# A hybrid transformer block on one core: the modulation product moved from the first mixer (TensorE) to the first MLP (VectorE), a third PSUM bank for the mixer's projections, later closing transposes of the first head, and matmuls on ones at the start

## The chip, the core and the metric

The kernel runs on one core of a Trainium2 chip. The core has five engines with an instruction queue each, which run in order: TensorE (PE, matrix products, with its weight loads shown as PEld), VectorE (DVE), ScalarE (ACT), GpSimd (POOL) and SyncE (SP, which here issues the DMA transfers). An instruction waits at the head of its queue until the semaphores that it needs are set, and everything behind it waits too. The metric is the device time of one execution in microseconds (us); lower is better.

## The reference

All data is fp32: `x` is 512 tokens by 1024. The reference is three stages one after the other:

```python
x = LN(alpha * x + mixer_gdn(x));  x = LN(alpha * x + mlp(x, 0))     # layer 0
x = LN(alpha * x + mixer_gla(x));  x = LN(alpha * x + mlp(x, 1))     # layer 1
mod   = silu(c) @ w_mod + b_mod         # one row of 3072: shift, scale, gate
mod_c = silu(c_ctx) @ w_mod + b_mod     # the same weights, 1024 x 3072
h  = rms(x)   * (1 + scale)   + shift
hc = rms(ctx) * (1 + scale_c) + shift_c  # ctx: 256 tokens
y = branches(h @ w_in, attention over hc and h) @ w_out;  out = x + gate * y
```

`mixer_gdn` is a gated delta rule with 8 heads in both directions: projections to q, k, v and z, a convolution of five taps over the tokens, triangular inverses within chunks of 64 tokens, a scan over chunks, a gated norm and an output projection. `mlp` is `relu(x w1)^2 w2` with 4096 hidden columns. The two modulation rows depend on `c`, `c_ctx` and `w_mod` alone, and nothing needs them before the context's normalisation, which runs beside the first MLP.

## The kernel before, in words

Products of fp32 are made as three products of halves: each operand is split into a rounded part (`hi`) and a rest (`lo`), and `mm3` (lines 337 to 339) issues hi·hi, hi·lo and lo·hi into one PSUM bank. A weight comes as a 512 KB transfer into `raw` on SP's queue (L322), ACT writes `hi` (L310), POOL, or for the mixer's projections VectorE, subtracts to give `lo` (both L316).

The program is written with a framework that fixes the order of every engine's queue ahead of time, from the order in which instructions are emitted and from priorities. `Weave` runs generators in the background of a main generator: at each `yield` of the main one (a tick) each background generator advances at its own rate.

The first mixer, `gdn`, takes 0 to 521 us of the profiled span. Its main generator is `dense(h)` for heads 0 to 7, which runs the projections: `proj` makes 24 matmuls of 128x512 into one of two banks (`acc`), and `proj_conv` then reads that bank with one ACT and four VectorE instructions (L705, `y<-acc`), the convolution; only then is the bank free. In the background stand, for each head, `inverse(h)`: 31 steps of two short POOL instructions (L830 and L832; VectorE does them for head 7), closed by two VectorE transposes (L839, L843) which are pinned in program order; then `double(h)`, `scan(h, d)` (short matmuls `psw`, `pso`, `psr` with VectorE or ACT steps between), and `closing(h)` with `stats` and `finish`. The last head's `finish(7)` (L974, L977) runs within the second half of the output projection (`wout_half`).

`mod`, which makes the two modulation rows, is one more background generator, at rate 0.18 from head 1 on: 24 weights of 512 KB through `wload`, 96 matmuls of 128x512 (L1374) into a bank of their own (`psmod`, the one `held` bank), and per sixth of the row a copy by ACT (L1377), four VectorE transposes (L1382) and two additions (L1385, L1386).

The first MLP takes 521 to 880 us. `mlp` runs 8 blocks of `up` (four columns of 128 hidden units: 24 matmuls, `relu` on ACT, square on VectorE at L485, split on ACT and VectorE) and `wout_half` (whose results VectorE adds at L364 and L366, `zacc<-sm`). A generator `side` is advanced by `next(side, None)` five times per block; it holds `ctx_tile` (which needs the modulation) and `gla_consts`. Then follow `gla` (880 to 1200), the second MLP (1200 to 1545) and the attention block (to the end).

Of the kernel before, what the change touches and what calls it, by code (L numbers as in the profile page):

```python
# [7 lines left out]
F32 = mybir.dt.float32  # L8
# [134 lines left out]
def _prep(inputs):  # L143
    g = {k: np.asarray(v) for k, v in inputs.items()}
    A = {}
    A["cst"] = _consts()
    A["chunk"], A["blocks"] = _chunk(), _blocks()
    x = g["x"][0]
    A["x"] = np.ascontiguousarray(x.reshape(4, 128, 1024).transpose(1, 0, 2))
    A["xT"] = np.ascontiguousarray(x.T.reshape(8, 128, 512).transpose(1, 0, 2))  # L150
    wa = g["a_w_in"][0]
    w4 = wa[:, :4096].reshape(1024, 4, 8, 128)
    w4 = w4[:, [1, 0, 2, 3]].transpose(0, 2, 1, 3).reshape(1024, 4096)
    A["wa"] = _lay_in(np.ascontiguousarray(w4))
# [12 lines left out]
    wb = g["b_w_in"][0]  # L167
    wk, wq = (wb[:, o:o + 512].reshape(1024, 4, 1, 128) for o in (512, 0))
    wr = wb[:, 2048:3072].reshape(1024, 4, 2, 128)
    A["wb"] = _lay_in(np.ascontiguousarray(np.concatenate([wk, wq, wr], 2).reshape(1024, 2048)))  # L170
    A["wbv"] = np.ascontiguousarray(wb[:, 1024:2048].reshape(2, 4, 128, 4, 256).transpose(3, 0, 2, 1, 4))
    A["wgl"] = np.ascontiguousarray(wb[:, 3072:].reshape(8, 128, 32).transpose(1, 0, 2))
    w2 = g["b_gate_w2"][0]
    w2x = np.zeros((128, 4, 2, 2, 128), np.float32)
    for d in range(2):
        for r in range(0, 128, 32):
            w2x[r + 16 * d:r + 16 * d + 16, :, 0, d] = w2[d].reshape(16, 4, 128)
        for r in (0, 32):
            w2x[r, :, 1, d] = g["b_gate_b"][0, d].reshape(4, 128)
    w2x = w2x.reshape(128, 4, 512)  # L180
    A["w2x"] = w2x
    A["wbo"] = _lay_out(g["b_w_out"][0])
    prm.append(_cols(g["b_norm_g"][0]))
    A["gsum"] = _gla_sums()
    A["grest"] = _gla_rest()
    A["rowA"] = np.concatenate([g["a_alog"].reshape(-1), g["a_dt_bias"].reshape(-1)])[None]
    prm += [_cols(g[n]) for n in ("norm_g_2", "b_mod_2", "c_2", "c_ctx_2", "q_lora_g_2", "kv_lora_g_2")]
    prm += [_cols(g[n][0, :128]) for n in ("q_norm_g_2", "k_norm_g_2")] + [_cols(g["pool_scale_2"])]
    sw = np.arange(64).reshape(2, 2, 16)[:, ::-1].reshape(-1)
    A["grow"] = np.stack([r for n in ("q_norm_g_2", "k_norm_g_2") for r in (g[n][0, 128:], g[n][0, 128:][sw])])  # L190
    A["rope"] = _rope()
    A["edge"] = _edge()
    A["ctx"] = np.ascontiguousarray(g["ctx_2"][0].reshape(2, 128, 1024).transpose(1, 0, 2))
    A["wmod"] = _lay_out(g["w_mod_2"][0])
    wi = g["w_in_2"][0]
    A["wu1"] = np.ascontiguousarray(wi[:, :448].reshape(4, 2, 128, 448).transpose(0, 2, 1, 3))
    A["wuc"] = np.ascontiguousarray(wi[:, 256:448].reshape(8, 128, 192).transpose(1, 0, 2))
    A["wi"] = _lay_in(np.ascontiguousarray(wi[:, 448:]))
    uq = g["w_uq_2"][0].reshape(2, 128, 4, 192).transpose(2, 1, 0, 3).reshape(4, 128, 384)
    ukv = g["w_ukv_2"][0].reshape(128, 4, 256).transpose(1, 0, 2)  # L200
    A["wqkv"] = np.ascontiguousarray(np.concatenate([uq, ukv], 2))
    A["wpool"] = np.ascontiguousarray(g["w_pool_2"][0].transpose(1, 0, 2))
    A["wo"] = _lay_out(g["w_out_2"][0])
    A["prm"] = np.ascontiguousarray(np.concatenate(prm, 1))
    return A
# [51 lines left out]
class Kern:  # L257
# [211 lines left out]
    def mlp(self, i, xT, after, early, side=iter(()), nb=8):  # L469
# [40 lines left out]
        for b in range(nb):  # L510
            nxt = up(b + 1) if b < nb - 1 else None
            if b == nb - 2:
                self.extra = None
            next(side, None)
            g = self.wout_half(prev, I[f"w2_{i}"], b, self.zacc, after if b == nb - 1 else None, b == 0,
                               pool=self.wp2, ps_of=self.sm)
            for n, _ in enumerate(g):
                if b == nb - 2 and n == 9:
                    early()
            prev = nxt  # L520
        st.close()


    def lead(self, xraw, xT):
# [2 lines left out]
        nc, I = self.nc, self.I  # L527
        mm = nc.tensor.matmul
        A_, V, G = nc.scalar, nc.vector, nc.gpsimd
        raw = self.wp.tile([128, 8, 128], F32, tag="raw", name="raw")  # L530
        G.memset(raw[:, :, 64:128], 0.0)
        for j in range(2):
# [14 lines left out]
            self.split(xT[0][:, q], xT[1][:, q], xraw[:, q], A_, V)  # L547
        w1 = self.wload(I["wa"][1])
        self.load_consts()
        psb = self.sm("psb")  # L550
        ps = [self.acc(), self.acc()]
        for k in range(8):
            for i in range(2):
# [7 lines left out]
    def gdn(self, xraw, xT, after):  # L561
# [105 lines left out]
        def emit_et(h):  # L667
            et = etb[:, h % 3]
            ET[h] = et
            for d in range(2):  # L670
# [5 lines left out]
                for t in range(4):  # L676
                    A_.activation(out=et[:, d * 4 + t], in_=ps[:, t * 128:(t + 1) * 128], func=AF.Exp,
                                  bias=negc[:, d, t, h:h + 1])

        def proj(w):  # L680
            ps = self.acc()
            for k in range(8):
                self.mm3(ps, (w[0][:, k], w[1][:, k]), (xT[0][:, k], xT[1][:, k]), k == 0, k == 7)
                if k % 2 == 1 and k < 7:
                    yield
            return ps
# [120 lines left out]
        def inverse(h):  # L807
# [20 lines left out]
            for j in range(31):  # L828
# [4 lines left out]
                                op=ALU.subtract)  # L833
                if j % 4 == 3:
                    yield
            t32 = ip.tile([128, 8, 8, 4], F32, name="t32")
            t32s[h] = t32
            pin = tc.keep_in_program_order if h < 7 else (lambda i: i)
# [157 lines left out]

        for h in range(8):
            if h == 1:
                md = wv.add(self.mod(one, t2), 0.18, high=False)
            wv.run(dense(h))  # L1000
        oTs.append(self.big([128, 2, 4, 512], "oTb", FR))
        zacc = self.big([128, 4, 1024], "zacc")
# [347 lines left out]
        a, w = o[name]  # L1350
        return self.prm[:, a:a + w]

    def mod(self, pool, t2):

        nc, I = self.nc, self.I
        V, A_, G = nc.vector, nc.scalar, nc.gpsimd
        mm = nc.tensor.matmul
        mc = self.pers["mc"] = self.cp.tile([128, 24, 2], F32, name="mc")
        g1 = self.pers["g1"] = self.cp.tile([128, 8, 2], F32, name="g1")
        sc = pool.tile([128, 2, 8], F32, name="sc")  # L1360
        A_.activation(out=sc.rearrange("p a b -> p (a b)"), in_=self.o2("c"), func=AF.Silu)
        st4 = pool.tile([128, 156], FR, name="st4")
        V.memset(st4.bitcast(F32), 0.0)
        s4 = st4[:, 0:32].rearrange("p (k j) -> p k j", j=4)
        for i in range(2):
            self.split(s4[:, :, 2 * i], s4[:, :, 2 * i + 1], sc[:, i], A_, V)
        for n in range(6):
            ps = self.held("psmod")
            for kk in range(4):
                w = self.wload(I["wmod"][kk, n])  # L1370
                yield
                for k in range(2):
                    for i in range(2):
                        mm(ps, lhsT=st4[:, 4 * (2 * kk + k):4 * (2 * kk + k) + 128], rhs=w[i][:, k],  # L1374
                           start=(kk + k + i == 0), stop=(kk + k + i == 5))
            row = t2("row").rearrange("p a b -> p (a b)")
            A_.activation(out=row[0:32], in_=ps[0:32], func=AF.Copy)  # L1377
            yield
            rt = t2("rt")
            rv = row[0:32].rearrange("p (j g i) -> p g j i", g=4, i=32)  # L1380
            for g in range(4):
                V.transpose(out=rt[32 * g:32 * g + 32, :, 0:32], in_=rv[:, g])  # L1382
            p2 = rt[:, :, 8:10]
            r2 = rt[:, :, 0:4].rearrange("p j (a b) -> p j a b", b=2)
            V.tensor_tensor(out=p2, in0=r2[:, :, :, 0], in1=r2[:, :, :, 1], op=ALU.add)  # L1385
            V.tensor_tensor(out=mc[:, 4 * n:4 * n + 4], in0=p2,  # L1386
                            in1=self.o2("b_mod")[:, 4 * n:4 * n + 4].unsqueeze(2).to_broadcast([128, 4, 2]), op=ALU.add)
            yield
        V.scalar_tensor_tensor(out=g1, in0=mc[:, 8:16], scalar=1.0,
                               in1=self.o2("norm_g").unsqueeze(2).to_broadcast([128, 8, 2]), op0=ALU.add, op1=ALU.mult)  # L1390
        yield
# [458 lines left out]
def build(ctx, tc, I, O):  # L1850
# [22 lines left out]
        pass  # L1873

    def side():
        for t in range(2):
            yield from K.ctx_tile(t, cpool)
        yield from K.gla_consts(cpool)
# [44 lines left out]
```

## Time and profile before

| | |
|---|---|
| median of 3 runs | 1821.02 us (1817.97 to 1821.89) |
| the profiled execution | 1817.16 us, of which its span 1815.4 us |
| PE busy | 1698.1 us, 94% of the span |
| DVE / ACT / POOL busy | 1029.0 / 798.3 / 805.9 us (57 / 44 / 44%) |
| mean granted TensorE clock | 0.969 of full speed |

A busy share is the time in which an engine executed something, so idle time is what is left. "[12.27 <-DVE y]" behind a row means that the engine stood idle 12.27 us before that instruction and that the last thing it waited for was a VectorE instruction that writes `y`.

### The profile page before, as it was taken

The numbers are of one execution on the slowest core, as the hardware profiler recorded it, in microseconds if no ns is written. First come the engines' busy times: TensorE is split into PE (matmuls) and PEld (weight loads), VectorE is DVE, ScalarE is ACT, GpSimd is POOL, SyncE is SP. The second block draws the span as 40 slices with busy tenths as digits, with TensorE's granted clock in tenths as the row PEclk, the third lists the DMA queues.
The fourth block names the chain that finished last, engine by engine and source line by source line (L and its number), as shares of the span: only waits on it lengthen the run. The fifth ranks groups of instructions, "written<-read, shape, count | busy, mean of one in ns | idle before, by whom it ended". The sixth has DMA issues, their size and how long they took to land.

```text
span 1815.4 us, 24657 instructions
## 1 busy us (share of the span) xinstructions
PE 1698.1 (94%) x9258; PEld 1409.3 (78%) x9258; DVE 1029.0 (57%) x2076; ACT 798.3 (44%) x1625; POOL 805.9 (44%) x840
## 2 busy tenths in 40 slices
PE   7698998898889999999999999889999999889998
PEld 6576876677678888888888888688888888778887
DVE  5467676685575344442756566664333345756684
ACT  6465665753534232222265645323222332556541
POOL 1567566634734444443243323634444444354431
PEclk9799989999899999999999999999999999999999
DMA  5121222013533233221221111322222223021111
GB/s 180 35 93 62 79 70 70 13 60 126 185 124 105 93 105 117 94 93 61 58 74 60 58 41 70 130 88 93 93 97 101 95 100 109 12 67 50 47 59 47
DMA packets 49559, 150.54 MB, mean 83 GB/s; under 512 B 11296, under 2 KB 12192, under 8 KB 49312
## 3 DMA queue, kind: packets, MB, share of 16 engines
q1 hardware_dynamic: 49296, 148.83, 23.8%
q8 instruction: 73, 1.20, 0.3%
q14 instruction: 46, 0.38, 0.1%
q10 hardware_dynamic: 144, 0.13, 0.0%
HBM read 146.85 MB, written 2.10 MB: 82 GB/s over the span
## 4 chain that ended last, share of the span: by engine, by line
PE 69%; POOL 10%; DVE 7%; issue 6%; ACT 5%; DMA 1%; POOLq 0%; SPq 0%; ACTq 0%; DVEq 0%
PE acc L337 12%; PE acc L339 12%; PE acc L338 11%; PE sm L337 6%; PE sm L339 6%; PE sm L338 6%; POOL lo L316 3%; POOL tm L830 3%; POOL ts L832 3%; PE psx L1173 1%; PE pst L345 1%; DVE zacc L451 1%; PE psc L1235 1%; ACT hi L310 1%; PE psmod L1374 1%
## 5 line engine op out<-in xcount | busy, mean ns | idle before, releaser
L316 POOL TENSOR_TENSOR lo<-raw,hi 128x1024 fp32r<-128x1024 f32 (+1 forms) x220 | 515.5, 2353 | 657.1 <-ACT hi L310 621.3
L310 ACT ACTIVATE hi<-raw 128x1024 fp32r<-128x1024 f32 (+2 forms) x248 | 260.0, 1050 | 440.0 <-PE sm L339 190.9
L337 PE MATMUL acc<-xh,hi 128*128 128x512 f32 (+1 forms) x976 | 380.7, 390 | 21.9 <-DVE y L705 14.3
L338 PE MATMUL acc<-xl,hi 128*128 128x512 f32 (+1 forms) x976 | 372.6, 382 | 0.0
L339 PE MATMUL acc<-xh,lo 128*128 128x512 f32 (+1 forms) x976 | 372.3, 381 | 0.0
L337 PEld LDWEIGHTS acc<-xh,hi 128*128 128x128 f32 x976 | 188.9, 194 | 55.4 <-issue 12.7
L339 PEld LDWEIGHTS acc<-xh,lo 128*128 128x128 f32 x976 | 187.9, 192 | 32.2
L338 PEld LDWEIGHTS acc<-xl,hi 128*128 128x128 f32 x976 | 188.8, 193 | 29.5
L485 DVE TENSOR_TENSOR r<-r 128x512 f32<-128x512 f32 x56 | 130.6, 2333 | 134.4 <-ACT r L484 134.3
L337 PE MATMUL sm<-hi,aT 128*128 128x512 f32 x496 | 196.5, 396 | 0.0
L339 PE MATMUL sm<-hi,aT 128*128 128x512 f32 x496 | 195.7, 395 | 0.0
L338 PE MATMUL sm<-lo,aT 128*128 128x512 f32 x496 | 194.8, 393 | 0.0
L366 DVE TENSOR_TENSOR zacc<-sm,zacc 128x512 f32<-128x512 f32 x112 | 76.0, 688 | 146.8 <-PE sm L339 146.8
L339 PEld LDWEIGHTS sm<-hi,aT 128*128 128x128 f32 x496 | 93.3, 188 | 22.0
L338 PEld LDWEIGHTS sm<-lo,aT 128*128 128x128 f32 x496 | 93.3, 188 | 21.4
L337 PEld LDWEIGHTS sm<-hi,aT 128*128 128x128 f32 x496 | 93.4, 188 | 20.6
L310 ACT ACTIVATE aT<-r 128x512 fp32r<-128x512 f32 x64 | 40.5, 632 | 144.2 <-DVE r L485 133.4
L830 POOL TENSOR_TENSOR tm<-ts,spare 128x54 f32<-128x54 f32 (+24 forms) x217 | 73.2, 337 | 47.4 <-DVE ts L825 17.4
L832 POOL TENSOR_TENSOR ts<-ts,tm 128x54 f32<-128x54 f32 (+24 forms) x217 | 72.2, 332 | 16.9
L705 DVE SCALAR_TENSOR_TENSOR y<-acc,prm,y 128x511 f32<-128x511 f32 (+1 forms) x96 | 70.6, 736 | 6.8 <-ACT y L702 5.8
L316 DVE TENSOR_TENSOR aT<-r,aT 128x512 fp32r<-128x512 f32 x64 | 46.8, 731 | 41.2 <-ACT aT L310 41.2
L316 DVE TENSOR_TENSOR lo<-raw,hi 128x1024 fp32r<-128x1024 f32 (+1 forms) x34 | 44.5, 1309 | 19.8 <-ACT hi L310 16.4
(482 smaller groups left out, 3344.9 us busy)
## 6 DMA issues: line engine op xcount, KB each, us to landing
raw<-in_w SPq DMA_DIRECT2D x128, 512.0 KB, 3.5
raw<-in_wa SPq DMA_DIRECT2D x31, 512.0 KB, 3.5
raw<-in_wmod SPq DMA_DIRECT2D x24, 512.0 KB, 3.6
raw<-in_wb SPq DMA_DIRECT2D x16, 512.0 KB, 3.5
raw<-in_wi SPq DMA_DIRECT2D x12, 512.0 KB, 3.5
raw<-in_wao SPq DMA_DIRECT2D x8, 512.0 KB, 3.5
rows<-in_lnr SPq DMA_DIRECT2D x8, 512.0 KB, 4.8
raw<-in_wbv SPq DMA_DIRECT2D x8, 512.0 KB, 3.4
```

The source lines that it names most:

```text
L310: e_hi.activation(out=hi, in_=src, func=AF.Copy)
L316: e_lo.tensor_tensor(out=lo[:, sl], in0=src[:, sl], in1=hi[:, sl].bitcast(F32), op=ALU.subtract)
L337: mm(ps, lhsT=l[0], rhs=r[0], start=start, stop=False)
L338: mm(ps, lhsT=l[0], rhs=r[1], start=False, stop=False)
L339: mm(ps, lhsT=l[1], rhs=r[0], start=False, stop=stop)
L345: self.nc.tensor.transpose(ps[:, t * 128:(t + 1) * 128], src(t), ident)
L366: V.tensor_tensor(out=zz, in0=ps, in1=zz, op=ALU.add)
L451: V.scalar_tensor_tensor(out=z[:, sl], in0=z[:, sl], scalar=rs, in1=self.ln_rows[:, 1, sl], op0=ALU.mult, op1=ALU.add)
L485: V.tensor_tensor(out=r, in0=r, in1=r, op=ALU.mult)
L705: V.scalar_tensor_tensor(out=y[:, a:b], in0=ps[:, a + sh:b + sh], scalar=conv[:, j, ct:ct + 1], in1=y[:, a:b], op0=ALU.mult, op1=ALU.add)
L830: E.tensor_tensor(out=tm[:, 0:k, 0:n], in0=ts[:, 0:k, j:j + 1].to_broadcast([128, k, n]), in1=ab[:, j + 1:32, j].unsqueeze(1).to_broadcast ...
L832: E.tensor_tensor(out=ts[:, 0:k, j + 1:32], in0=ts[:, 0:k, j + 1:32], in1=tm[:, 0:k, 0:n], op=ALU.subtract)
```

## The change

It has four parts. (1) `mod` is no longer in the mixer's background; it is the first thing in `side`, in the first MLP. There the weights come as 24 transfers of 512 KB to tiles `wm` (two buffers, `ch` and `cx`, of the pool that `ctx_tile` uses), unsplit. VectorE multiplies and sums them with the silu of `c` and of `c_ctx` as per-partition factors, into a PSUM bank (`modacc`): 8 instructions of 128x256 per transfer for the first 16 transfers and 4 for the last 8, 160 in all. Per pair of transfers it copies the sums to SBUF (`part`, 12 copies), 40 fp32 matmuls of two columns with a matrix of ones sum over the partitions, and 20 small additions write `mc`. For that `next(side, None)` is called three more times in each `wout_half` but the last, so eight times per block. (2) In `proj`, every third projection takes the bank that `psmod` had (`acc3`). (3) `inverse(0)` yields seven times more before its closing transposes. (4) The kernel begins with 16 matmuls of 128x512 on ones, whose result is never read.

```diff
@@ mlp
             for n, _ in enumerate(g):
                 if b == nb - 2 and n == 9:
                     early()
+                if b < nb - 1 and n in (3, 8, 13):
+                    next(side, None)
@@ gdn, its first lines
+        busy = self.b16.tile([128, 512], FR, tag="b16", name="busy")
+        V.memset(busy.bitcast(F32), 1.0)
+        psb = self.sm("psb")
+        for _ in range(16):
+            mm(psb, lhsT=busy[:, 0:128], rhs=busy, start=True, stop=True)
@@ proj
-            ps = self.acc()
+            banks[0] += 1
+            ps = self.held("acc3") if banks[0] % 3 == 1 else self.acc()
@@ inverse
+            for _ in range(7 if h == 0 else 0):
+                yield
             t32 = ip.tile([128, 8, 8, 4], F32, name="t32")
@@ the loop over heads
             if h == 1:
-                md = wv.add(self.mod(one, t2), 0.18, high=False)
+                self.mod_open()
@@ mod (a part of the old one, then of the new one)
-                w = self.wload(I["wmod"][kk, n])
-                yield
-                for k in range(2):
-                    for i in range(2):
-                        mm(ps, lhsT=st4[:, 4 * (2 * kk + k):4 * (2 * kk + k) + 128], rhs=w[i][:, k],
-                           start=(kk + k + i == 0), stop=(kk + k + i == 5))
+        def load(i):
+            raws[i] = pool.tile([128, 4, 256], F32, tag=("ch", "cx")[i % 2], name="wm")
+            nc.sync.dma_start(out=raws[i], in_=I["wmod"][i // 2, i % 2])
+
+        def sums(n, nv, part):
+            ps = self.sm("psmod")
+            for v in range(nv):
+                for j in range(2):
+                    nc.tensor.matmul(ps[:, 2 * (2 * v + j):2 * (2 * v + j) + 2], lhsT=part[:, v, j * 128:(j + 1) * 128],
+                                     rhs=self.c("ones")[:, 0:2], start=True, stop=True)
+            for v in range(nv):
+                V.tensor_tensor(out=mc[:, 2 * n:2 * n + 2, v], op=ALU.add, ...
...
+        for n in range(12):
+            nv = 2 if n < 8 else 1
+            ps = self.held("modacc").rearrange("p (v c) -> p v c", v=2)
+            for kk in range(2):
+                w = raws.pop(2 * n + kk)
+                for k in range(4):
+                    for v in range(nv):
+                        f = self.sc[:, v, 4 * kk + k:4 * kk + k + 1]
+                        if kk + k == 0:
+                            V.tensor_scalar(out=ps[:, v], in0=w[:, k], scalar1=f, scalar2=None, op0=ALU.mult)
+                        else:
+                            V.scalar_tensor_tensor(out=ps[:, v], in0=w[:, k], scalar=f, in1=ps[:, v], op0=ALU.mult, op1=ALU.add)
+                if 2 * n + kk + 2 < 24:
+                    load(2 * n + kk + 2)
+                if kk == 0 and done:
+                    sums(*done)
                 yield
+            part = pool.tile([128, 2, 256], F32, tag=("xr", "cw")[n % 2], name="part")
+            V.tensor_copy(out=part[:, 0:nv], in_=ps[:, 0:nv])
+            done = (n, nv, part)
@@ side
+        yield from K.mod(cpool)
         for t in range(2):
             yield from K.ctx_tile(t, cpool)
```

The order on VectorE in the first head, before, from the last transpose ahead of `inverse(0)`'s steps (`spare<-acomp`) to its closing transposes (`t<-ts`, `tt<-t`). `y<-acc` are the convolutions, four rows of instructions to a projection.

```order
L821 STREAM_TRANSPOSE spare<-acomp 128x1024
L705 SCALAR_TENSOR_TENSOR y<-acc,prm,y 128x510 x2
L779 TENSOR_TENSOR vn<-pst,nk 128x512
L316 TENSOR_TENSOR lo<-raw,hi 128x1024
L705 SCALAR_TENSOR_TENSOR y<-acc,prm,y 128x511 x2
L705 SCALAR_TENSOR_TENSOR y<-acc,prm,y 128x510
L839 STREAM_TRANSPOSE t_736<-ts 128x8x8x4
L705 SCALAR_TENSOR_TENSOR y<-acc,prm,y 128x510
```

The same place after the change (`acc_609` is the third bank):

```order
L831 STREAM_TRANSPOSE spare<-acomp 128x1024
L715 SCALAR_TENSOR_TENSOR y<-acc,prm,y 128x510
L715 SCALAR_TENSOR_TENSOR y<-acc_609,prm,y 128x511
L316 TENSOR_TENSOR lo<-raw,hi 128x1024
L715 SCALAR_TENSOR_TENSOR y<-acc_609,prm,y 128x511
L715 SCALAR_TENSOR_TENSOR y<-acc_609,prm,y 128x510 x2
L316 TENSOR_TENSOR lo<-raw,hi 128x1024
L715 SCALAR_TENSOR_TENSOR y<-acc,prm,y 128x511
L725 TENSOR_SCALAR ssk<-ssk 128x4
L715 SCALAR_TENSOR_TENSOR y<-acc,prm,y 128x511
L759 RECIPROCAL rk<-ssk 128x4
L715 SCALAR_TENSOR_TENSOR y<-acc,prm,y 128x510
L851 STREAM_TRANSPOSE t_863<-ts 128x8x8x4
```

Before, five `y` instructions stand between the two transposes; now eight do, and the last of a convolution stands behind `t<-ts` in both.

SP's queue around the end of the mixer, before: the weights of the output projection (`in_wao`), the residual (`in_x`), the modulation's (`in_wmod`) and the first MLP's (`in_w_0`).

```order
L322 DMA raw<-in_wao 128x1024 x2
L1003 DMA zacc<-in_x 128x4096
L322 DMA raw<-in_wmod 128x1024 x8
L322 DMA raw<-in_wao 128x1024 x4
L322 DMA raw<-in_w_0 128x1024 x4
L424 DMA rows<-in_lnr 128x1024 x2
```

After:

```order
L322 DMA raw<-in_wao 128x1024 x6
L1015 DMA zacc<-in_x 128x4096
L322 DMA raw<-in_wao 128x1024 x2
L322 DMA raw<-in_w_0 128x1024 x4
L424 DMA rows<-in_lnr 128x1024 x2
L322 DMA raw<-in_w_0 128x1024
L1381 DMA wm<-in_wmod 128x1024 x2
L322 DMA raw<-in_w_0 128x1024 x6
L424 DMA rows<-in_lnr 128x1024 x2
L1381 DMA wm<-in_wmod 128x1024
```

Eight modulation loads are gone from ahead of the last four `in_wao`, and all 24 now stand among the first MLP's weights.

VectorE's queue at the start of the first MLP, after (before, the rows of `modacc` and `part` are not there and the others follow each other directly): `r<-r` is the square, `aT<-r,aT` the split of the hidden units.

```order
L504 TENSOR_TENSOR r<-r 128x512
L1409 SCALAR_TENSOR_TENSOR modacc<-wm,sc,modacc 128x256 x2
L316 TENSOR_TENSOR aT<-r,aT 128x2x256
L1409 SCALAR_TENSOR_TENSOR modacc<-wm,sc,modacc 128x256 x5
L1416 COPY part<-modacc 128x512
L1407 TENSOR_SCALAR modacc<-wm,sc 128x256 x2
```

The sums stand in bursts between a square and the split that needs it, and between that split and the next square.

## Rows read from the trace of the kernel before

**Rows 1.** The page's first two parts: busy time, share and instructions of each engine, and PE's busy tenths in 40 slices of 45.4 us.

```profile
PE 1698.1 (94%) x9258; PEld 1409.3 (78%) x9258; DVE 1029.0 (57%) x2076; ACT 798.3 (44%) x1625; POOL 805.9 (44%) x840
...
PE   7698998898889999999999999889999999889998
```

**Rows 2.** Windows by stage: from and to, length, busy us (and instructions) of PE, PEld, DVE, ACT and POOL, PE's granted clock, share of the DMA engines, GB/s.

```profile
24.00:84.00 60.00, 40.24 (x171) 32.20 (x169) 27.41 (x64) 31.26 (x68) 23.60 (x65) 0.82 0.18 59
84.00:287.00 203.00, 188.16 (x1249) 147.66 (x1250) 135.65 (x283) 124.21 (x344) 132.74 (x278) 0.93 0.21 73
287.00:424.00 137.00, 115.67 (x874) 93.28 (x872) 99.72 (x249) 78.10 (x226) 67.06 (x141) 0.91 0.15 52
424.00:521.00 97.00, 79.99 (x450) 62.52 (x451) 64.65 (x111) 42.46 (x87) 62.59 (x32) 0.92 0.44 159
545.00:587.00 42.00, 42.00 (x198) 34.91 (x198) 22.97 (x23) 18.32 (x27) 20.11 (x9) 1.00 0.30 103
587.00:629.00 42.00, 42.00 (x190) 34.92 (x189) 17.50 (x17) 13.57 (x20) 16.41 (x8) 1.00 0.25 86
629.00:880.00 251.00, 251.00 (x1114) 206.43 (x1113) 106.68 (x122) 70.20 (x93) 96.90 (x45) 1.00 0.28 96
```

**Rows 3.** What PE waited for between 24 and 424 us: instruction and releaser, us in total, times, longest.

```profile
PE acc L337 <- DVE y L705: 14.3, 4, 12.3
PE psmod L1374 <- POOL lo L316: 10.8, 5, 6.4
PE psw L937 <- DVE r L924: 7.2, 3, 5.8
PE psf L862 <- DVE t L839: 5.0, 1, 5.0
PE acc L337 <- ACT spare L770: 4.0, 1, 4.0
...
PE psmod L1374 <- ACT hi L310: 1.3, 1, 1.3
```

**Rows 4.** Timelines of PE, VectorE and POOL in the first head, two stretches: start, length, engine, line, operation, [idle before, releaser].

```profile
56.52 0.80 PE L337 MATMUL acc<-xh,hi 128*128 128x512 f32 x1 [4.00 <-ACT spare L770]
...
83.90 0.77 PE L337 MATMUL acc<-xh,hi 128*128 128x512 f32 x1 [12.27 <-DVE y L705]
...
82.68 0.45 DVE L839 STREAM_TRANSPOSE t<-ts 128x256 f32<-128x256 f32 x1 [13.08 <-POOL ts L832]
83.05 0.71 DVE L705 SCALAR_TENSOR_TENSOR y<-acc,prm,y 128x510 f32<-128x510 f32 x1
...
82.43 0.22 POOL L832 TENSOR_TENSOR ts<-ts,tm 128x8 f32<-128x8 f32 x1
```

**Rows 5.** Windows again, of the modulation's matmuls (L1374) alone: in each stretch the busy us of PE (and their count), then of PEld.

```profile
84.00:287.00 203.00, 18.11 (x48) 9.31 (x48) 0.93 0.21 73
287.00:424.00 137.00, 3.19 (x8) 1.67 (x8) 0.91 0.15 52
424.00:455.00 31.00, 2.19 (x8) 1.50 (x8) 1.00 0.36 130
455.00:475.00 20.00, 10.38 (x32) 5.36 (x32) 1.00 0.48 158
```

**Rows 6.** Timelines of POOL ahead of 287 us (the `lo` of a modulation weight), of PE there, and of PE at 414 us.

```profile
281.04 2.36 POOL L316 TENSOR_TENSOR lo<-raw,hi 128x1024 fp32r<-128x1024 f32 x1
...
293.30 0.80 PE L937 MATMUL psw<-r,tt 128*128 128x128 f32 x2 [5.80 <-DVE r L924]
...
414.33 0.28 PE L862 MATMUL psf<-t,spare 32*32 32x32 f32 x2 [5.00 <-DVE t L839]
```

**Rows 7.** Timelines of PE and VectorE in the mixer's tail: the last head's first `psw`, its last `pso` and the transposes of `finish(7)`.

```profile
454.52 0.61 PE L937 MATMUL psw<-vn,tt 128*128 128x128 f32 x4
...
473.43 0.38 PE L955 MATMUL pso<-y,etb 128*128 128x128 f32 x2
...
484.08 0.47 PE L977 MATMUL pst<-cst,oa 128*128 128x128 f32 x1 [2.74 <-DVE oa L974]
...
469.10 2.30 DVE L1385 TENSOR_TENSOR rt<-rt 128x8 f32<-128x8 f32 x1
...
478.50 1.39 DVE L967 TENSOR_SCALAR fo<-sso 128x4 f32<-128x4 f32 x1
...
481.20 2.82 DVE L974 TENSOR_TENSOR oa<-oa,fo 128x512 f32<-128x512 f32 x1 [1.05 <-POOL fo L970]
```

**Rows 8.** Timeline of PE at the start: the second matmul, and where the distance from one to the next falls.

```profile
8.57 0.80 PE L554 MATMUL psb<-xl,hi 128*128 128x512 f32 x1 [0.42 <-DVE xl L316]
...
13.43 0.63 PE L337 MATMUL acc<-xh,hi 128*128 128x512 f32 x1
13.86 0.54 PE L338 MATMUL acc<-xl,hi 128*128 128x512 f32 x1
14.23 0.40 PE L339 MATMUL acc<-xh,lo 128*128 128x512 f32 x1
14.47 0.40 PE L554 MATMUL psb<-xh,hi 128*128 128x512 f32 x1
14.70 0.40 PE L554 MATMUL psb<-xl,hi 128*128 128x512 f32 x1
```

**Rows 9.** Timelines of VectorE in `gla` (four instructions of the kind and size of the sums, with a PSUM operand; seven that follow each other on one tile), and of PE in the attention block (12 fp32 matmul records).

```profile
932.83 1.65 DVE L1222 SCALAR_TENSOR_TENSOR S<-S,et,pss 128x256 f32<-128x256 f32 x4
...
936.22 2.33 DVE L1242 COPY_PREDICATED P<-kt_mask,psc 128x128 f32<-128x128 uint8 x7
...
1644.78 1.60 PE L1776 MATMUL pso<-v,pt 128*128 128x128 f32 x12 [0.28 <-DVE kn L1678]
```

**Rows 10.** Duration of one of those of L1222 (its line's view: least/median/most ns, first and last start), and the page's group of the MLP's additions into `zacc`: busy us, mean ns of one, idle before and releaser.

```profile
L1222 DVE SCALAR_TENSOR_TENSOR S<-S,et,pss x16: 467/471/481, 932.8 to 1119.2; 128x256 f32<-128x256 f32 x16
...
L366 DVE TENSOR_TENSOR zacc<-sm,zacc 128x512 f32<-128x512 f32 x112 | 76.0, 688 | 146.8 <-PE sm L339 146.8
```

**Rows 11.** What ACT waited for in the first MLP (521 to 880 us), and SP's queue in 545 to 700 us.

```profile
ACT hi L310 <- PE sm L339: 90.8, 27, 8.6
...
ACT hi L310 <- PE acc L338: 38.3, 24, 4.3
...
ACT hi L310 <- DMA raw<-in_wb: 6.2, 2, 4.8
...
SPq L322 <- POOL lo L316: 127.0, 25, 10.4
```

More of the change, by code (lines that the diff above doesn't have):

```diff
@@ L193, in _prep @@
     A["ctx"] = np.ascontiguousarray(g["ctx_2"][0].reshape(2, 128, 1024).transpose(1, 0, 2))
-    A["wmod"] = _lay_out(g["w_mod_2"][0])
+    A["wmod"] = np.ascontiguousarray(g["w_mod_2"][0].reshape(2, 4, 128, 12, 256).transpose(3, 0, 2, 1, 4))
     wi = g["w_in_2"][0]
@@ L549, in lead @@
         self.load_consts()
-        psb = self.sm("psb")
         ps = [self.acc(), self.acc()]
@@ L678, in emit_et @@
                                   bias=negc[:, d, t, h:h + 1])
+        banks = [0]
         def proj(w):
-            ps = self.acc()
+            banks[0] += 1
+            ps = self.held("acc3") if banks[0] % 3 == 1 else self.acc()
             for k in range(8):
@@ L1351, in o2, with mod_open, mod @@
         return self.prm[:, a:a + w]
-    def mod(self, pool, t2):
+    def mod_open(self):
+        self.sc = self.cp.tile([128, 2, 8], F32, name="sc")
+        self.nc.scalar.activation(out=self.sc.rearrange("p a b -> p (a b)"), in_=self.o2("c"), func=AF.Silu)
+    def mod(self, pool):
         nc, I = self.nc, self.I
-        V, A_, G = nc.vector, nc.scalar, nc.gpsimd
-        mm = nc.tensor.matmul
+        V = nc.vector
         mc = self.pers["mc"] = self.cp.tile([128, 24, 2], F32, name="mc")
@@ L1359, in mod @@
         g1 = self.pers["g1"] = self.cp.tile([128, 8, 2], F32, name="g1")
[L1360 to L1364, printed above, removed]
-        for i in range(2):
[L1366 to L1369, printed above, removed]
-                w = self.wload(I["wmod"][kk, n])
-                yield
-                for k in range(2):
-                    for i in range(2):
-                        mm(ps, lhsT=st4[:, 4 * (2 * kk + k):4 * (2 * kk + k) + 128], rhs=w[i][:, k],
-                           start=(kk + k + i == 0), stop=(kk + k + i == 5))
-            row = t2("row").rearrange("p a b -> p (a b)")
-            A_.activation(out=row[0:32], in_=ps[0:32], func=AF.Copy)
-            yield
[L1379 to L1388, printed above, removed]
@@ new lines, in mod @@
+        raws = {}
+        def load(i):
[8 more added lines that the diff above has]
+            for v in range(nv):
+                V.tensor_tensor(out=mc[:, 2 * n:2 * n + 2, v], op=ALU.add,
+                                in0=ps[:, 4 * v:4 * v + 4].rearrange("p (j e) -> p j e", e=2)[:, :, 0],
+                                in1=self.o2("b_mod")[:, 2 * n:2 * n + 2])
@@ new lines, in mod @@
+        for i in range(2):
+            load(i)
+        yield
+        done = None
+        for n in range(12):
[14 more added lines that the diff above has]
+                    sums(*done)
+                yield
+            part = pool.tile([128, 2, 256], F32, tag=("xr", "cw")[n % 2], name="part")
+            V.tensor_copy(out=part[:, 0:nv], in_=ps[:, 0:nv])
+            done = (n, nv, part)
@@ L1389, in mod @@
+        yield
+        sums(*done)
         V.scalar_tensor_tensor(out=g1, in0=mc[:, 8:16], scalar=1.0,
```

## The prediction, made before the changed kernel was run

> **What bounds the kernel now.** I read the busy shares first, then the windows by stage, the waits of PE, the timelines around its longest gaps, and for the MLP the rows of VectorE. PE is busy 94% of the span, and its 40 slices are full except at the start, in the first mixer (the first 11 slices or so) and around `gla` [rows 1]. The windows say where PE's idle time lies in the mixer: 19.8 us of 60 in 24 to 84, 14.8 of 203 in 84 to 287, 21.3 of 137 in 287 to 424, 17.0 of 97 in 424 to 521; in the first MLP, 545 to 880, it has none [rows 2]. So the mixer gains both from matmuls taken out and from waits taken out, and in the MLP each thing that PE does more costs its full time. PE's clock in the mixer is 0.82 to 0.93 of full speed, in the MLP 1.00 [rows 2]: matmuls behind a gap run at 1.2 instead of 2.4 GHz for a while, 0.427 us from one to the next where the others take 0.228 (13.43 to 13.86, and 14.47 to 14.70 [rows 8]).
>
> **The stall of the first head.** PE stands 12.27 us before 83.90, for a `y` of VectorE [rows 4]. That `y` is the last of a convolution, and it stands in VectorE's queue behind the pinned transpose `t<-ts`, which waited 13.08 us for POOL's last step of `inverse(0)` at 82.43. PE needs the bank that this `y` reads. In the changed order eight `y` stand ahead of that transpose and not five, and one whole convolution of them reads the third bank. That is one projection more, 24 x 0.228 = 5.5 us of PE's work, plus what the extra ticks let VectorE do first. Here PE has a gap of 4.00 us before 56.52 too, for ACT reading a bank [rows 4]; with three banks PE has another to write. I count 12.27 + 4.00 and 3 us for some 15 matmuls behind the gaps at 0.427 instead of 0.228, and leave 4 of it for what the inverse still holds back: **-15** (between -6, where one projection is all that is gained, and -19).
>
> **Modulation out of the mixer.** Of the 96 matmuls 56 lie before 424 us, with 21.3 us of busy time [rows 5]; a record's end reaches over the next one's start, so the path loses less: at least 56 x 0.228 = 12.8. I take **-17**. PE waited 10.8 us for the `lo` of these weights and 1.3 for their `hi` [rows 3]; during such a wait the other engines catch up, so I take **-10** of 12.1 (0 if they were all cover for a chain). A `lo` of 2.36 us at 281.04, and one like it 6 us earlier, stand on POOL ahead of the mask whose result the scan at 293.30 needed, where PE waited 5.80 us [rows 6]: **-4** (0 to -4.7). The wait of 5.00 us at 414.33 is head 7's inverse on VectorE [rows 6], which shared SBUF with other work: **-1**.
>
> **Start.** 16 matmuls on ones run while the input is on its way; after them the first matmuls can be at 2.4 GHz. Before, 13 distances of 0.427 lie between 8.57 and 14.23 [rows 8]; at 0.228 they would save 2.6, if the splits of `x` keep pace: **-1.5** (0 to -2.6).
>
> **What takes the place of those waits.** All that is taken out brings the chains (inverse, doubling, scan) and VectorE nearer to PE. VectorE is busy 136 us of 203 and 100 of 137 in the mixer's middle [rows 2], so 66 and 73%; with the same work in some 40 us less it would be at about 77%. Waits for VectorE are the largest in the list that remains (7.2 for `r`, 5.0 for `t` [rows 3]). I charge **+12** (0, if the queues just move together, to +30, which would be as much as the waits removed above).
>
> **Mixer's tail.** From the last head's first `psw` at 454.52 to the first transpose of `finish(7)` at 484.08 it takes 29.6 us [rows 7]. In that stretch PE runs 32 of the modulation's matmuls, 10.4 us of busy time [rows 5], VectorE a 2.30 us addition of it (L1385) in front of the last `r` [rows 7], and the output projection waits for weights behind eight modulation loads in SP's queue. Without these the scan's own chain is some 12 us (four steps) and the statistics and the scaling 5.5 to 8, since `oa` there took 2.82 us and `fo` 1.39 while POOL made `lo` [rows 7]. So 18.5 instead of 29.6, -11, and -2 for the eight before 455 (2.19 busy): **-13** (-6, if the other half's matmuls fill the same time, to -17).
>
> **First MLP.** PE gets 40 fp32 products, each in two records; 12 such records took 1.60 us [rows 9]; with 0.38 for the last one, as for a `pso` [rows 7], their distance is (1.60 - 0.38)/11 = 0.11, so 80 x 0.11 = **+9** (5, where a record of two columns is half as long, to 10). VectorE gets 160 sums. Four of that kind and size took 1.65 us, one of them 0.471, hence (1.65 - 0.471)/3 = 0.393 from one to the next [rows 9, 10]. The first 16 bursts of eight are spread over two blocks: 128 x 0.393 = 50.3, eight copies of some 0.7 (taken as `zacc`'s 0.688 [rows 10]) and 16 additions of some 0.15: 58 us. With VectorE's own 22.97 + 17.50 [rows 2] this is 99 in 84 us, plus what PE gets there (32 products, 7 us) and the calls' spread, about 95. VectorE is then full for two blocks and ends some 4 us late: **+4** (0, since a backlog of an MLP column can lie in the three `r` buffers; 17, if the sums take longer). The blocks after that have 2.6 us of sums a call and less, and space: 106.7 busy of 251 us [rows 2]. The 24 loads are in SP's queue anyway, before and after, without the `hi` and `lo` that they had: ACT and POOL lose 24 of each.
>
> The sum: -1.5 - 15 - 17 - 10 - 4 - 1 + 12 - 13 + 9 + 4 = -36.5 against the profiled run's own time of 1817.2, so 1780.7. The median of the runs lies 3.9 above that run; I give the runs a third of that, **1782**.
>
> **A rule against the row.** The distance of 0.393 us between sums is shorter than one's duration of 0.471 [rows 9, 10], so an instruction starts before the last one's end is recorded. The Trainium skill, in "VectorE: DVE Perf Modes", section "The DRAIN you can't avoid", says that the next VectorE instruction doesn't start before the pipeline is empty. By that the distance would be a full duration; the row at hand doesn't agree, but its four write apart, and the sums follow on one bank.
>
> **Rivals.**
> *The gain is swallowed.* The waits removed come back as waits for VectorE and the scan: +30 instead of +12 in the mixer: 1800. For it: 7.2 us for `r` and 66 to 73% VectorE [rows 2, 3]. Against it: PE's own work there falls by 17 us in any case.
> *VectorE bounds the first MLP.* If sums that follow on one bank take their whole 0.471 us, it is 160 x 0.078 = 12.5 us more in a stretch that is full: 1794. For it: with one row `v` alone, the last 32 depend on each other. Against it: seven instructions on one tile took 2.33 us at 0.30 each, a distance of about 0.34 [rows 9], longer than one by little. What the Trainium skill says in the section named above would make this case of it.
> *Slower: the loads hold SP's queue.* A `wm` load waits at its head until VectorE has finished the burst that read its buffer, and every weight of the MLP behind it waits too. If each of the 24 made PE wait for a weight for 2.5 us: +60, 1842. It decides against the change from (36.5 + 3.6)/24 = 1.7 us a load. Against it: ACT's `hi` waited for PE's use of buffers 90.8 + 38.3 us and for a transfer only in two cases of another stage [rows 11], so weights come early; SP itself already waits 127 us for POOL's `lo` [rows 11], which is room.
> *More than forecast.* No new waits in the mixer and a tail at its own chain: -12 and -4 more, and the clock stays up: under 1757 if all hold.
>
> **How the numbers follow.** Forecast 0.62 (its own range 1765 to 1797); swallowed 0.16 (1793 to 1810); VectorE in the MLP 0.10 (1790 to 1800); the loads 0.06 (over 1824); more than forecast 0.06 (under 1757). The range 1757 to 1808 leaves out the last two and a part of the second, 0.16 in all. About 0.2%, 3.6 us, is what a measurement of this kernel can tell from no change; under 1817 lie all cases but the loads and an edge of the second: faster 0.91, same 0.03, slower 0.06.
>
> **What would show it.** Right: no PE gap over 5 us in 70 to 90 us; no `psmod` in the mixer; first to last `psw` of the tail and `finish(7)` within 20 us; the first MLP longer by 9 to 17 us with VectorE at over 90% in its first two blocks, and PE there without waits for a weight. Wrong: a new PE wait of several us per head in the mixer, a sum distance over 0.47 us, or PE waiting in the MLP for `hi` behind SP.

## The result, and the profile after

The changed kernel takes 1841.9 us (median, 1838.3 to 1848.6) against 1821.45: **1.2% slower**, ratio 1.0119 [1.0087, 1.0152]. 1782 was forecast. The profiled execution took 1848.6, the slowest of the four, and its span is 1846.7; the one before (1817.16) lies at the fast end of its runs, so the two spans are 31 us apart where the medians are 20. Its windows, with the bounds and columns of [rows 2]:

```profile
24.00:84.00 60.00, 44.98 (x223) 36.43 (x221) 35.25 (x72) 35.93 (x87) 23.12 (x65) 0.92 0.20 71
84.00:287.00 203.00, 161.46 (x1128) 131.85 (x1129) 110.04 (x247) 107.57 (x303) 85.30 (x222) 0.87 0.13 45
287.00:424.00 137.00, 105.93 (x772) 83.86 (x771) 80.88 (x215) 68.51 (x210) 69.88 (x180) 0.83 0.07 24
545.00:587.00 42.00, 42.00 (x267) 38.00 (x266) 36.99 (x67) 17.55 (x25) 17.11 (x8) 1.00 0.53 185
587.00:629.00 42.00, 42.00 (x197) 34.85 (x196) 38.34 (x74) 10.62 (x14) 16.60 (x8) 1.00 0.46 157
```

PE is busier than before up to 84 us (44.98 for 40.24) and then much idler: 41.5 us without work in 84 to 287, where it had 14.8, and 31.1 in 287 to 424, where it had 21.3. The modulation's matmuls are gone from there, and PE waits instead. The list of its waits, 24 to 560 us (as [rows 3], which end at 424):

```profile
PE acc L337 <- DVE y L715: 49.8, 5, 17.3
PE pst L345 <- ACT vT L717: 16.3, 1, 16.3
PE psf L874 <- DVE t L851: 10.4, 2, 6.5
```

No wait for a modulation weight is left, but the wait for `y` has grown from 14.3 to 49.8 us in five places. They aren't in the first head: two of them are

```profile
188.89 0.79 PE L337 MATMUL acc<-xh,hi 128*128 128x512 f32 x1 [12.77 <-DVE y L715]
...
248.27 0.80 PE L337 MATMUL acc<-xh,hi 128*128 128x512 f32 x1 [17.32 <-DVE y L715]
```

What `y` waits for is seen on VectorE and POOL. Their timelines around the second head's inverse, and where the next inverse begins and ends:

```profile
121.38 0.22 POOL L842 TENSOR_TENSOR ts<-ts,tm 128x8 f32<-128x8 f32 x1
...
153.39 0.74 DVE L715 SCALAR_TENSOR_TENSOR y<-acc,prm,y 128x510 f32<-128x510 f32 x1
154.05 0.43 DVE L851 STREAM_TRANSPOSE t<-ts 128x256 f32<-128x256 f32 x1
...
155.65 0.29 DVE L835 COPY ts<-blk 128x256 f32<-128x256 f32 x1
...
156.57 0.28 POOL L840 TENSOR_TENSOR tm<-ts,spare 128x31 f32<-128x31 f32 x1
...
181.24 0.22 POOL L842 TENSOR_TENSOR ts<-ts,tm 128x8 f32<-128x8 f32 x1
...
183.86 0.31 ACT L826 ACTIVATE bc<-spare 32x128 f32<-32x128 f32 x1 [13.86 <-POOL spare L810]
...
186.11 0.41 DVE L828 STREAM_TRANSPOSE acomp<-bc 128x128 f32<-128x128 f32 x1 [13.92 <-ACT bc L826]
```

POOL's last step of `inverse(1)` ends at 121.6, but the transpose `t<-ts` stands behind the `y` of two more convolutions in VectorE's queue (counted below) and runs at 154.05, 32 us later. Only behind it comes the copy that fills `ts` for `inverse(2)`, which runs from 156.57 to 181.5. The mask of the next inverse stands behind it on POOL (`spare`, L810), the copies on ACT and the transposes `acomp` on VectorE wait for that mask, two `y` of a convolution stand behind `acomp`, and PE waits for them until 188.89. So POOL's inverse and PE's projections take turns where before they overlapped. Before, the same pair is

```profile
133.52 0.22 POOL L832 TENSOR_TENSOR ts<-ts,tm 128x8 f32<-128x8 f32 x1
...
143.96 0.44 DVE L839 STREAM_TRANSPOSE t<-ts 128x256 f32<-128x256 f32 x1
```

10 us apart. For the heads 1 to 5 the transposes follow POOL's last step by 10, 11, 20, 18 and 0 us before and by 32, 36, 33, 15 and 16 after; that of head 6 comes at 360.6 before and at 388.7 after, though the second inverse had begun 9 us sooner (95.7 for 104.7).

The first MLP came out near the forecast +13: from the first product of its second matrix (at 586.30 after, 569.68 before) to the last (911.76, 885.49) it takes 325.5 us for 315.8, 9.6 more; PE has no wait in 560 to 905 us.

### The profile page after: what moved, and what is told of

It is laid out like the page before. It is cut to its first block, busy times and chain, and to the rows that moved or that the text cites. A ratio compares the mean times of both kernels' runs of the same rounds, so it can differ in the third digit from the quotient of the medians.

```text
span 1846.7 us, 24751 instructions
## 1 busy us (share of the span) xinstructions
PE 1692.7 (92%) x9258; PEld 1410.2 (76%) x9258; DVE 1069.5 (58%) x2230; ACT 774.4 (42%) x1593; POOL 743.6 (40%) x816
## 4 chain that ended last, share of the span: by engine, by line
PE 64%; POOL 13%; issue 10%; DVE 6%; ACT 5%; DMA 1%; POOLq 0%; SPq 0%; ACTq 0%; DVEq 0%
PE acc L337 11%; PE acc L338 11%; PE acc L339 11%; PE sm L337 6%; PE sm L339 6%; PE sm L338 6%; POOL tm L840 4%; POOL ts L842 4%; POOL lo L316 2%; PE psx L1185 1%; PE pst L345 1%; PE psc L1247 1%; DVE zacc L451 1%; PE pso L1807 1%; PE pso L967 1%
## 5 line engine op out<-in xcount | busy, mean ns | idle before, releaser
L316 POOL TENSOR_TENSOR lo<-raw,hi 128x1024 fp32r<-128x1024 f32 (+1 forms) x196 | 457.4, 2344 | 641.1 <-ACT hi L310 637.7
L337 PE MATMUL acc<-xh,hi 128*128 128x512 f32 (+1 forms) x976 | 377.9, 387 | 50.1 <-DVE y L715 49.8
L310 ACT ACTIVATE hi<-raw 128x1024 fp32r<-128x1024 f32 (+2 forms) x224 | 234.6, 1048 | 390.8 <-PE sm L339 165.9
L485 DVE TENSOR_TENSOR r<-r 128x512 f32<-128x512 f32 x56 | 115.1, 2054 | 111.9 <-ACT r L484 111.9
L842 POOL TENSOR_TENSOR ts<-ts,tm 128x54 f32<-128x54 f32 (+24 forms) x217 | 68.3, 315 | 17.0
L1409 DVE SCALAR_TENSOR_TENSOR modacc<-wm,sc,modacc 128x256 f32<-128x256 f32 x140 | 68.2, 487 | 4.5 <-DMA wm<-in_wmod 0.9
```

What stands on the lines that cost most here:

```text
L310: e_hi.activation(out=hi, in_=src, func=AF.Copy)
L316: e_lo.tensor_tensor(out=lo[:, sl], in0=src[:, sl], in1=hi[:, sl].bitcast(F32), op=ALU.subtract)
L337: mm(ps, lhsT=l[0], rhs=r[0], start=start, stop=False)
L485: V.tensor_tensor(out=r, in0=r, in1=r, op=ALU.mult)
L842: E.tensor_tensor(out=ts[:, 0:k, j + 1:32], in0=ts[:, 0:k, j + 1:32], in1=tm[:, 0:k, 0:n], op=ALU.subtract)
L1409: V.scalar_tensor_tensor(out=ps[:, v], in0=w[:, k], scalar=f, in1=ps[:, v], op0=ALU.mult, op1=ALU.add)
```

## The experiments

The order that the framework gave VectorE, without any time, shows what each part does to the closing transposes. Convolutions (four `y` each) that stand ahead of `t<-ts` of heads 0 to 7:

```
before                                 3.75   9     11  15  18     20  22.5   24
the change                             5.75  11     14  17  19.25  21  23     24
 without the yields           (e1)     5.75   9     11  14  18     20  23.25  24
 without the third bank       (e2)     5     11     14  17  19     21  22.75  24
 without both                 (e3)     3.5    9     11  14  18     20  22.5   24
before, with the yields alone (e4)     6     11     14  17  19     21  23     24
 inverses 1 to 3 at rate 0.8  (e5)     5.75   8.75  11  14  17     20  23.25  24
 transposes not pinned        (e6)     5.75   8.75  11  14  17     20  23.5   24
 e1, 0 to 3 at rate 0.8       (e7)     5.75   7.5   10  14  17     20  23.25  24
 two yields                   (e9)     5.75   9     11  17  17     21  23.5   24
 four yields                  (e10)    5.75   8.25  11  17  19.25  21  23     24
```

In the changed kernel the yields move nothing in the first head, for which they are written: 5.75 with and without them (with two banks they do: 5 for 3.5 in e2 and e3, 6 for 3.75 in e4). They move heads 1 to 3 by two or three convolutions and heads 4 and 5 by about one, because each `inverse` begins in program order after the one before (`after=[last[0]]`) and the rate of 0.55 leaves the late one no room to catch up (e5 tests this).

**Four variants that take parts away.** e1 and e2 undo one part each:

```diff
-            for _ in range(7 if h == 0 else 0):      # e1, e3
-                yield
-            banks[0] += 1                             # e2, e3
-            ps = self.held("acc3") if banks[0] % 3 == 1 else self.acc()
+            ps = self.acc()
```

e3 undoes both, e4 is the kernel before with the two lines of the yields added. ("The row" in what follows is the chain of inverses of all heads.)

> The change without the seven additional yields in inverse(0). Theory A (the yields push the closing transposes of heads 0 to 3 behind two or three more convolutions in VectorE's queue, each next inverse starts only after the transposes of the one before, and so the row of inverses ends some 25 us later): the mixer's tail comes 40 to 65 us sooner than in the changed kernel, the transposes of heads 1 to 3 follow within 20 us on POOL's last step instead of 32 to 36, and the whole takes 1780 to 1800 us. Theory B (the modulation's matmuls only filled time in which PE waits for the inverses anyway, so taking them out gains nothing): at most 10 us less than the changed kernel, 1830 or more. Theory C (the third bank lets PE run ahead and brings the waits): the same as B, with the waits for y still near 50 us.

> The change with two banks for the projections instead of three. Theory A: still slow, within 10 us of the changed kernel (1832 to 1852), since the transposes stand as late as there. Theory B: the same or a little slower. Theory C: 20 us or more faster than the changed kernel.

> Modulation moved and the matmuls at the start, without the third bank and without the yields. Theory A: faster than before, 1785 to 1805 us; the stall of the first head near 72 to 84 us is back at about 12 us. Theory B: within 8 us of before, or slower by the 10 us that the first MLP costs. Theory C: like A.

> The kernel before with nothing but the seven yields in inverse(0). Theory A: slower than before by 15 to 35 us, with transposes of heads 1 to 3 late by 20 us or more after POOL's last step. Theory B: within 8 us of before, since the modulation's matmuls still fill the waits. Theory C: within 8 us of before.

All four ran on one chip, beside the kernel before at 1825.5:

| | median, us | ratio to before |
|---|---|---|
| e1, without the yields | 1775.1 | 0.9732 [0.9702, 0.9763] |
| e2, without the third bank | 1845.4 | 1.0126 [1.0094, 1.0157] |
| e3, without both | 1794.7 | 0.9847 [0.9818, 0.9876] |
| e4, the yields alone | 1854.9 | 1.0173 [1.0146, 1.0199] |

Theory A holds in all four, e1 with more than it said: 1775.1 for 1780 to 1800, and the tail (the first transpose of `finish(7)` on PE, 430.7 for 499.7) 69 us sooner for 40 to 65. B and C fall: B in e1, e3 and e4, C in e1, e2 and e4. In e1 the transposes of head 1 run 7 us after POOL's last step, and POOL begins the next inverse 1 us after that:

```profile
122.06 0.22 POOL L842 TENSOR_TENSOR ts<-ts,tm 128x8 f32<-128x8 f32 x1
...
129.26 0.43 DVE L849 STREAM_TRANSPOSE t<-ts 128x256 f32<-128x256 f32 x1
...
130.27 0.26 POOL L840 TENSOR_TENSOR tm<-ts,spare 128x31 f32<-128x31 f32 x1 [5.95 <-DVE ts L835]
```

and PE is busy again in the mixer's middle (186.4 of 203 us, and 123.5 of 137):

```profile
84.00:287.00 203.00, 186.44 (x1333) 148.56 (x1334) 136.31 (x306) 121.14 (x346) 120.10 (x314) 0.94 0.13 48
287.00:424.00 137.00, 123.51 (x979) 99.26 (x974) 89.68 (x243) 75.37 (x231) 58.63 (x101) 0.98 0.16 59
```

The end of the row holds nearly all of the difference. The closing transpose of the last head, in e1 and then in the change:

```profile
374.32 0.45 DVE L849 STREAM_TRANSPOSE t<-ts 128x256 f32<-128x256 f32 x1
...
439.14 0.45 DVE L851 STREAM_TRANSPOSE t<-ts 128x256 f32<-128x256 f32 x1
```

It comes 64.8 us later. In all twelve kernels of this document what is left of the profiled span behind that transpose is 1394 to 1408 us, while the spans reach from 1771 to 1850.

The parts don't add. Without the yields the third bank gives 19.6 us (e3 to e1); with them no gain can be told (1845.4 in e2, 1841.9 in the change, on two chips, and the intervals of the two ratios overlap). Moving the modulation, with the matmuls at the start, gives 31 us without the yields (before to e3), and 9.5 with them (e4 to e2). That much of theory B is true: once the row of inverses sets the pace, PE's work taken out mostly lengthens PE's waits.

**Is it the row, or the first head's transposes themselves, and is it their place in the queue?** Two variants keep the yields:

```diff
-            last[0] = wv.add(inverse(h), 0.55 if h < NZ else 1.2, after=[last[0]], high=True)
+            last[0] = wv.add(inverse(h), (0.55 if h == 0 else 0.8) if h < NZ else 1.2, after=[last[0]], high=True)   # e5
-            pin = tc.keep_in_program_order if h < 7 else (lambda i: i)
+            pin = lambda i: i                                                                                        # e6
```

> The whole change, yields included, but the inverses of heads 1 to 3 advance at 0.8 per tick instead of 0.55. Theory A (what costs is that the row of all later inverses is late, not that the first head's transposes are): most of the 67 us between the changed kernel and the one without yields comes back, 1772 to 1795 us, and POOL's inverses 1 to 3 are followed by their transposes within 12 us. Rival A2 (the first head's own late transposes cost, through everything that waits for them): 1830 or more.

> The whole change, yields included, but no transpose is pinned in program order: the framework may set them ahead of convolutions that were emitted earlier. Theory A: the yields cost only because the pinned transposes stand behind convolutions that wait for PE, so 1772 to 1800 us. Rival A2: 1830 or more, since the yields also hold back the steps of the inverses themselves.

e5 took 1775.4 us, ratio 0.9744 [0.9725, 0.9763], e6 1776.7, 0.9739 [0.9724, 0.9753]: each gives back the whole loss, as A expected, with the seven yields in place. In e5 the transposes of heads 1 to 3 follow POOL's last step by 0, 2 and 9 us. In e6 the second head's transpose runs as soon as POOL is done:

```profile
120.53 0.22 POOL L842 TENSOR_TENSOR ts<-ts,tm 128x8 f32<-128x8 f32 x1
...
120.78 0.45 DVE L851 STREAM_TRANSPOSE t<-ts 128x256 f32<-128x256 f32 x1 [9.41 <-POOL ts L842]
```

So neither late steps nor the first head's late end cost the time, but that the pinned transposes of the later heads stand behind convolutions for which PE has yet to work. (What unpinning gives without the yields was not run.)

**Can the row be drawn closer, and what are the matmuls at the start worth?** e7 is e1 with 0.8 in place of 0.55 for heads 0 to 3; e8 is e1 without the memset and the 16 matmuls.

> The change without the yields, and all inverses of heads 0 to 3 at 0.8 per tick instead of 0.55. If the row of inverses still sets the mixer's end when each follows as early as it can, it ends sooner: 1760 to 1772 us. If what is left is PE's own work and the scans, no change from the kernel without the yields, 1770 to 1780.

> The change without the yields and without the matmuls on ones at the start. By the sum of the prediction 1.5 us slower than with them (1774 to 1780 us), PE's first 13 distances at 0.427 us again; if a start at the low clock shifts later gaps, up to 5 us slower.

e7 took 1782.1 us, 0.9771 [0.9757, 0.9786], outside both expectations: some 7 us slower than e1. Here a transpose stands too early. Head 1's has 7.5 convolutions ahead of it where e1's has 9, so it stands within a convolution, and VectorE comes to it before POOL has finished:

```profile
122.45 0.45 DVE L849 STREAM_TRANSPOSE t<-ts 128x256 f32<-128x256 f32 x1 [13.69 <-POOL ts L842]
122.82 0.70 DVE L715 SCALAR_TENSOR_TENSOR y<-acc,prm,y 128x510 f32<-128x510 f32 x1
```

The `y` behind it waits as long, and PE has a new wait of 13.4 us for the `kq` that is made from it, until 125.42. It is the stall of the first head [rows 4] once more, in the second. `inverse(3)` starts at 189.1 where e1's starts at 175.9. e8 took 1775.7, 0.9738 [0.972, 0.9757]: the matmuls on ones make no difference that can be measured, and only some 6 of the first distances are long, not 13 (last section).

**Does the loss grow with the yields or with the transposes moved?** The change with 2 and with 4 instead of 7.

> The whole change with two yields in inverse(0) instead of seven. In VectorE's order only head 3's transposes move, from behind 14 convolutions to behind 17 (heads 1 and 2 stand as without yields). Theory A: head 3's transposes come some 20 us later than without yields, of which the 18 us that the fourth inverse had to wait anyway hide most: 1775 to 1795 us. Rival A3 (the cost grows with the number of yields, whatever the order): 1775 + 2/7 of 67 = 1794 us, 1790 to 1800.

> The whole change with four yields instead of seven. Heads 3 and 4 are moved behind 17 and 19.25 convolutions, heads 1 and 2 are as without yields. Theory A: two of the four transposes are late, the first of them hidden in part: 1785 to 1815 us. Rival A3: 1775 + 4/7 of 67 = 1813 us, 1808 to 1818.

e9 took 1794.0 us, 0.985 [0.9828, 0.9873], e10 1815.4, 0.9968 [0.9954, 0.9982]. e9 lies in the ranges of A and of A3, e10 in A3's and 0.4 us above A's (1785 to 1815), and A3's plain proportion (1794 and 1813) is nearer in both: the loss is 9.5, 10.1 and 9.5 us per yield with two, four and seven. The place in the queue still explains where it goes, but my size for e9 was wrong: I took 20 us for three convolutions, and head 3's transpose comes 41 us after POOL is done with that inverse (47 in e10):

```profile
199.39 0.22 POOL L842 TENSOR_TENSOR ts<-ts,tm 128x8 f32<-128x8 f32 x1
...
241.06 0.44 DVE L851 STREAM_TRANSPOSE t<-ts 128x256 f32<-128x256 f32 x1
...
243.35 0.44 POOL L840 TENSOR_TENSOR tm<-ts,spare 128x31 f32<-128x31 f32 x1
```

Of these 41 us some 18 were slack (in e1 `inverse(4)` begins at 220.1, 18 us after head 3's transpose at 202.3), which leaves 23: `inverse(4)` begins at 243.35, 23.2 us later than in e1, and the profiled spans differ by 1796.9 - 1773.9 = 23.0. "Whatever the order" is refuted by e5 and e6, which keep seven yields and lose nothing. That the loss goes with the yields as long as rate and pins stay as they are is not refuted by these three points; why it should, when at two yields mainly one head pays and at seven three do, stays open.

e1, e5, e6 and e8 stand at 1775 to 1777 us and beat both kernels; among themselves they can't be told apart.

## Why the prediction was wrong, point by point

**The step that failed is the third part of the change, priced within "the stall of the first head" at -15.** I read the order at the first head alone, saw eight `y` ahead of the transpose instead of five and counted "what the extra ticks let VectorE do first" as a gain. The third bank had made those eight; the yields' own price is **+67 us** (1841.9 - 1775.1, or some 70 by the ratios to the kernel before; +29 alone on the kernel before). The order that I had would have told: heads 1 to 3 stand two or three convolutions later, and [rows 4] showed that a convolution behind `t<-ts` waits for POOL; that a transpose behind convolutions makes POOL wait in turn, I didn't ask. The other parts together gave more than was forecast: with the yields taken out 50 us by the medians and 41.5 by the profiled spans, where the sum was 36.5. That 1775 lies so near 1782 is in part luck, as the terms below show.

**First head.** The wait was to be mostly gone. It isn't: PE stood 16.3 us before 85.56, and in e1 15.4 us before 84.56, since `inverse(0)` ends at the same time as before, near 84. The gain comes from what PE has done until then: its seventh projection starts at 56.1 instead of 83.9, its ninth at 88.6 instead of 103.6. -15 was forecast, 19.6 measured without the yields (e3 to e1), of which 11.0 are there at the ninth projection (88.9 for 99.9) and the rest comes in later heads: the size is near, but not by the wait that was to go.

**Modulation out of the mixer, with its tail and the new waits.** -17 - 10 - 4 - 1 + 12 - 13 is -33; with the first MLP's +13 and the start's -1.5 it makes -21.5. Measured: 31 less (before to e3). In the profiled executions the MLP's first `sm` product comes 31.0 us sooner in e3 (538.72 for 569.68), where -34.5 was forecast up to there, and 56.4 sooner in e1 (513.32), where -49.5 was. So the mixer's sum was right within 7 us in both, but not each of its terms. The tail was over-sized: from the last head's first `psw` to `finish(7)` it takes 21.9 us in e3 and in e1 for 29.6 before, 7.7 less where 11 was forecast. The new waits came in about the size that was charged: PE's waits in 24 to 560 us, without those for modulation weights, add up to 60.6 before and 69.9 in e3, 9 more for +12. That e3 gains 31 on the median in spite of the MLP's 9 is in part the spread of the runs (the profiled spans differ by 23.1).

**First MLP.** +13 forecast; 9.0 to 9.7 measured (e3 and the change). The products with the matrix of ones are nearly all of it. Eight records in the changed kernel:

```profile
585.26 0.39 PE L339 MATMUL acc<-xh,lo 128*128 128x512 f32 x1
585.49 0.95 PE L1387 MATMUL psmod<-cst,part 128*128 128x2 f32 x8
586.30 0.48 PE L337 MATMUL sm<-hi,aT 128*128 128x512 f32 x1
```

0.81 us from the first to the next product. The 12 groups together hold PE for 7.9 us, and after each the next distance is some 0.32 instead of 0.23, 1.1 in all: 9.0, as forecast. (The first group stands just ahead of the measured stretch, and eight transposes of `xr`, 0.8 us, that ran ahead of it before stand within it.) VectorE's +4 didn't come, though its sums were under-sized (last section) and it is busy 88 and 91% of the two windows (55 and 42% before [rows 2]). PE has no wait there; that the three `r` buffers took it, as the prediction had allowed, was not tested.

**The rivals.** *Swallowed* was the nearest in kind, a wait in place of the ones removed, but I bounded it at +30 and gave it no mechanism at the yields. *VectorE bounds the MLP* fell: the slower sums came, the stall didn't. *The loads hold SP's queue* gave 1842, which is the time that was measured, and fell all the same: SP waited 40.8 us for the sums in 560 to 720 us, and PE waited for nothing in 560 to 905. A right number is no evidence for its mechanism. *More than forecast* took 12 and 4 from 1782, which is 1766; the rest, down to 1757, was to come from the clock and had no sum behind it.

**Start.** -1.5 forecast, nothing measurable (e8 to e1: 0.6). The condition was "if the splits of `x` keep pace", and they don't: behind the ones PE is 0.23 us from one product to the next at once, but then waits for the halves of `x`, as in e1:

```profile
12.36 0.50 PE L561 MATMUL psb<-xl,hi 128*128 128x512 f32 x1 [0.65 <-DVE xl L316]
```

Its sixteenth product behind the ones starts at 13.39; without ones it starts at 12.84 (e8), 13.50 (e4) and 14.47 (before).

## What to carry to other kernels

Where background work is a chain (each piece begins after the one before) at a rate that just keeps up, a delay in the first piece is a delay in all: read the order at every later piece, not at the one for which the delay was written. Count for each closing instruction that is pinned in a queue what stands ahead of it and on which engine that waits: too late a place makes the chain wait (the change), too early a place makes what stands behind it wait (e7). Price the parts of a change apart before adding them: here one part cost more than the other three gained, and while its chain set the pace, the others were worth a third or less.

## What the runs showed of the hardware

A VectorE sum of 128x256 that reads a PSUM bank and writes the same bank follows the one before it by 0.525 us, longer than the 0.49 that is recorded for one:

```profile
563.55 3.64 DVE L1409 SCALAR_TENSOR_TENSOR modacc<-wm,sc,modacc 128x256 f32<-128x256 f32 x7
```

(3.64 - 0.49)/6 = 0.525. Four of the same size that write apart had 0.393 [rows 9, 10]. So the price per sum that I took was a quarter too low. It is not that one sum reads what the one before it wrote: the first two of a group (L1407) read no PSUM and write separate halves of the bank, and stand 1.01 - 0.49 = 0.52 apart too:

```profile
601.87 1.01 DVE L1407 TENSOR_SCALAR modacc<-wm,sc 128x256 f32<-128x256 f32 x2
```

In the trace's semaphore records each instruction of such a group but the first waits for a semaphore that the one before it sets. Over this whole trace, of 889 VectorE instructions that follow another without a gap and wait for no VectorE semaphore, 816 start 0.06 us or more before the recorded end of the one before; of 649 that wait for one, 370 start 0.02 to 0.05 us behind it (the others may wait for an older one). So the wait goes with the longer distance; a run that takes it out of the sums was not made. The Trainium skill ("VectorE: DVE Perf Modes", section "The DRAIN you can't avoid") says that the next instruction waits until the pipeline is empty, and that one which is not held starts earlier. The sums agree with the first half at 0.525 us, and the four of [rows 9], at 0.393, with the second; the prediction named the first half alone.

The first products of e8 and e4, which have no ones, stand 0.43 us apart at first, as those of the kernel before do [rows 8]: 512 columns in 0.427 us are 1.2 GHz. (The clock column of the windows shows 1.00 for 8 to 12 us in all three, so here the level is read from the distances.) The distance falls below 0.3 us 3.9 us after the first product in e8 (10.98), 3.8 us after it in e4 (11.32) and 6.9 us after it before (14.23), although e4 and the kernel before begin with the same instructions after 7.6 and 7.4 us of idle PE. How soon the clock rises thus differed from one execution to the next, and a gain at the start can't be counted on.
